# Three edits to a one-core transformer layer: separate PSUM banks in the seven-product quads, another order of the opening norms, earlier loads of the output projection's weights

## The chip, the cores and the metric

The kernel runs on one core of a Trainium2 chip. The metric is device time in microseconds (us); lower is better. The kernel before took 2078.35 us, the median of three runs (2078.32 to 2083.11).

## The reference

The kernel computes one layer of a hybrid decoder in float32: x of 1024 tokens by 1024 features, with 16 learned meta tokens ahead of them (1040 rows in all).

```python
h = h + 0.5 * swiglu(rms_norm(h, ffn1_norm), ffn1_w_in, ffn1_w_out)   # D_FF = 2816
u = rms_norm(h, mix_norm) @ w_in
o = concat[hgrn2(...4 heads, blocks of 128...), stick_breaking(...8 heads...)]
h = h + o @ w_out
h = h + 0.5 * swiglu(rms_norm(h, ffn2_norm), ffn2_w_in, ffn2_w_out)
# swiglu(h) = (silu(h @ w_in[:, :D_FF]) * (h @ w_in[:, D_FF:])) @ w_out
```

The output is h without the meta tokens.

## The kernel before, in words

**Products in three matmuls.** A float32 operand is held as two parts: a rounded high part (`wh`, `xh`, made by ScalarE's copy to fp32r at L268, L145 or L518) and the rest (`wl`, `xl`, made by VectorE's subtraction at L270, L147 or L520). A product of a 128-row piece is three matmuls: high by high, low by high, high by low. In `fast_in` three bufs each of `wh` and `wl` (and eight of `raw` in the first FFN, six in the second) let weights be prepared up to three products ahead of TensorE.

**Seven-product quads.** A 2x2 block product of the FFN's first matrix (`quad` in `fast_in`) is made from seven block products in place of eight: left operands are weight blocks a11, a21, a22, a12 or sums of them (s1 = a21 + a22, s2 = s1 - a11, a11 - a21, a12 - s2, made by GpSimd at L283), right operands are `B11, B21, B22, T1, T2, T3, T4`. TensorE works in the order B11, T2, B21, T3, T1, T4, B22; in quads that were begun early ("opened") the B11 and B21 products of six quads come first, and then T2, T3, T1, T4, B22 of one quad after the other. Each product is 12 matmuls and goes to a PSUM bank `qa` (B11, then B21 on top of it), `qb` (T2, then T3 and T4 on top of it) or `qc` (T1, then B22 on top). PSUM has two bufs each of `qa`, `qb`, `qc` and `qd`. VectorE or ScalarE reads a bank between two products that add up in it: `p1` is ScalarE's copy of B11 (L356), `u2 = p1 + qb` after T2 and `u3 = p1 + qb` after T3 (both L361). A matmul that adds to a bank waits until that read is over.

**The opening.** Tokens are in three blocks: block 0 of 272 columns ("plain", its products are ordinary ones into `qd`), blocks 1 and 2 of 384 columns each (the two halves of the quads). `run()` loads block 0's rows, norms them (`norm_rows`: per 128-row tile a square-sum, on VectorE for the second tile (L662) and else on ScalarE (L666), a square root on ScalarE (L667), a reciprocal (L670) and a multiplication of the row (L671) on VectorE), turns them by transposes on TensorE (L648) and makes `X`. Then 40 plain products of block 0 run (5 pairs of gate and up columns, L313 `qd<-X`), and between them, after products 12, 14, 16 and so on, six transposes of block 2's rows (evicted as `ba`, L692), then of block 1's (`bb`), while ScalarE and VectorE make the operands B and T (L219, L220, L705 to L718).

**What sets the order.** TensorE's order is written by hand (`manual_schedule(engines={nc.tensor.engine})`). ScalarE, VectorE, GpSimd and the DMA queue of SyncE are ordered by a list scheduler ahead of the run, by priority and by its own estimate of when things are ready; `high_priority()` raises a piece of code, and `issue_after(x)` puts it behind instruction x on its engines. On the chip each engine then goes strictly through its own list.

**The output projection.** `mix_out` runs first with the last four 128-row pieces of w_out (stick-breaking heads), which adds into `res` (L1640), then with the first four (the HGRN2 heads), which adds into `hm` (L1670). The weights of a half row of columns are four `raw` tiles (two bufs), cast at L145 and L147 into eight bufs of `wh` and `wl`. `ws[1]` are the weights of the second half of the columns, wanted from the third group of 12 matmuls of the second run on. HGRN2 head 3 is the last one; its output is `oH` (L965 on ScalarE, L966 on GpSimd) and is the fourth piece of each group. `from_dram` loads the `oT` tiles of the first run, two DMAs for each block.

Of the kernel before, what the change touches and what calls it, by code (L numbers as in the profile page):

```python
# [15 lines left out]
AF = mybir.ActivationFunctionType  # L16
# [4 lines left out]
P = 128  # L21
# [18 lines left out]
class Block:  # L40
# [212 lines left out]
    def fast_in(self, ops, n, w_in, actD, openers, ev0, open_ev, feed=None, plain=None,  # L253
# [19 lines left out]
        def block(i, h, col):  # L273
            t = self.wraw.tile([P, 4, P], F32, tag="raw", name="raw", bufs=self.in_bufs)
            nc.sync.dma_start(
                t, w_in[512 * h : 512 * h + 512, col + P * i : col + P * i + P]
                .rearrange("(k p) f -> p k f", p=P)
            )
            return t
# [58 lines left out]
        def quad(col, take, opened=None, also=None):  # L338
# [41 lines left out]
            u3 = kept("u3", p1, go("b", "T3", False))  # L380
            take(1, 1, go("c", "T1", True), u3)
            take(1, 0, go("b", "T4", False), p1)
# [273 lines left out]
    def norm_rows(self, ci, rows, junk):  # L656

        nc = self.nc
        for i, (row, at, m) in enumerate(rows):
            s, r = self.ss[:m, 3 * ci + i, 0:1], self.ss[:m, 3 * ci + i, 1:2]  # L660
            if i == 1:
                nc.vector.scalar_tensor_tensor(  # L662
                    junk[1][:m], row[:m], 1.0, row[:m], ALU.mult, ALU.mult, accum_out=s
                )
            else:
                nc.scalar.activation(junk[0][:m], row[:m], AF.Square, accum_out=s)  # L666
            self.root = nc.scalar.activation(  # L667
                r, s, AF.Sqrt, bias=self.eps[:m], scale=1.0 / D
            )
            nc.vector.reciprocal(r, r)  # L670
            nc.vector.tensor_scalar_mul(row[:m], row[:m], r)  # L671

    def first_plain(self, rows, junk, x):
# [3 lines left out]
        def evict(k, ps):  # L677
            g = self.g1[:, k : k + 1]
            hi, lo = x[0][:, k, :], x[1][:, k, :]
            nc.scalar.mul(hi, ps, g)  # L680
# [77 lines left out]
    def hgrn_fill(self, xh, xl, pool, dst):  # L758

        nc = self.nc  # L760
        nc.scalar.activation(self.lb, self.mx, AF.Sigmoid)
        nc.scalar.activation(self.lbc, self.mx, AF.Sigmoid, scale=-1.0)
# [574 lines left out]
    def run(self):  # L1337
# [20 lines left out]
        with ExitStack() as c0:  # L1358
            with ExitStack() as c1:
                with tc.manual_schedule(engines={nc.tensor.engine}), ExitStack() as c2:  # L1360
# [37 lines left out]
                    rows.append(self.rows_of(2, rp, nc.sync))  # L1398
                    drain(islice(steps, 4))
                    self.norm_rows(2, rows[1], junk)  # L1400
# [3 lines left out]
                    rows.append(self.rows_of(1, rp, nc.sync))  # L1404
                    self.norm_rows(1, rows[2], junk)
# [205 lines left out]
            with tc.manual_schedule(engines={nc.tensor.engine}):  # L1611
                right, cx, pre = ExitStack(), ExitStack(), ExitStack()
                with ExitStack() as c1:
# [10 lines left out]

                    def from_dram(b):
                        t = self.pool_o.tile([P, 2, 4, P], F32R, tag="oT", name="oT", bufs=3)
                        for i in range(2):
                            self.last_o = nc.sync.dma_start(
                                t.bitcast(F32)[:, i],
                                oD[:, :, i, b * P : b * P + P].rearrange("k p t -> p k t"),  # L1630
                            )
# [40 lines left out]
                    with tc.issue_after(self.last_o.ins):  # L1672
                        for b in range(2):
                            begin(0, b)
                        ws[1] = self.mix_weights(0, 1)
# [153 lines left out]
```

## Time and profile before

| | |
|---|---|
| median of three runs | 2078.35 us |
| lowest and highest run | 2078.32 and 2083.11 us |
| the profiled execution: its own time | 2084.77 us |
| the profiled execution: span from first to last instruction | 2083.1 us |
| TensorE busy | 2012.5 us (97%) |
| VectorE, ScalarE, GpSimd busy | 1377.7, 909.3, 636.5 us |
| mean granted TensorE clock | 0.995 |

The profile is one execution. Its rows give the start in us, a duration, the engine (PE is TensorE, PEld its weight loads, DVE VectorE, ACT ScalarE, POOL GpSimd, SPq SyncE's DMA queue), the line of the kernel, the operation, out and in, and in square brackets how long the engine had been idle and what released it. TensorE sets the time of nearly all stages; where it is idle or its clock is lowered, time is lost.

### The profile page before, as it was taken

Reading aid. Unit: us, or ns where it says so; the run is one execution under the profiler, and the core shown is the slowest. Engines: PE = TensorE matmul, PEld = TensorE weight load, DVE = VectorE, ACT = ScalarE, POOL = GpSimd, SP = SyncE. Lnnn points to the kernel's source line nnn. Section 1 sums busy time; section 2 is a strip of 40 time slices with the busy share of each in tenths; the row PEclk is TensorE's granted clock in tenths of the full one; section 3 lists DMA queues with packets and bytes.
Section 4 is the critical chain, followed back from the end, with each engine's and each line's share of the span. In section 5 each row is a group of like instructions: output and inputs, shape, how many; then the busy total and the mean of one; then the engine's idle time right before and its main releaser. Section 6 shows DMA issues by size and latency. Waiting matters only on the chain.

```text
span 2083.1 us, 31612 instructions
## 1 busy us (share of the span) xinstructions
PE 2012.5 (97%) x11249; PEld 1787.1 (86%) x11249; DVE 1377.7 (66%) x2073; ACT 909.3 (44%) x1864; POOL 636.5 (31%) x696
## 2 busy tenths in 40 slices
PE   7899999999999999999999998999999999999999
PEld 7899999999987899988887878878778888878887
DVE  6767754546688842257878757648667667667774
ACT  7743333334564534456566624336223323334443
POOL 2256644452000002243433300210555445431000
PEclk9999999999999999999999999999999999999999
DMA  8453322226875745435453262674333333239573
GB/s 240 134 179 114 110 93 85 96 86 213 282 219 172 234 134 168 150 116 131 123 140 108 68 215 92 203 258 132 105 123 107 96 107 112 91 138 351 188 227 112
DMA packets 289647, 314.96 MB, mean 151 GB/s; under 512 B 24080, under 2 KB 218000, under 8 KB 289488
## 3 DMA queue, kind: packets, MB, share of 16 engines
q1 hardware_dynamic: 272304, 260.83, 40.4%
q0 software_dynamic: 16144, 52.10, 6.6%
q8 instruction: 89, 1.46, 0.3%
q14 instruction: 70, 0.57, 0.1%
q10 hardware_dynamic: 1040, 0.00, 0.0%
HBM read 228.62 MB, written 84.23 MB: 150 GB/s over the span
## 4 chain that ended last, share of the span: by engine, by line
PE 78%; DVE 5%; ACT 2%; issue 1%; DMA 1%; POOL 0%; SPq 0%; DVEq 0%; ACTq 0%; POOLq 0%
PE o L599 17%; PE qb L313 13%; PE qc L313 8%; PE qa L313 8%; PE proj L162 5%; PE proj L160 5%; PE proj L161 5%; PE qd L313 3%; PE wo L1252 3%; PE o L561 3%; PE flip L1071 2%; PE lvl L840 2%; DVE keep L1217 1%; PE oacc L1141 1%; PE oacc L1143 1%
## 5 line engine op out<-in xcount | busy, mean ns | idle before, releaser
L313 PE MATMUL qb<-T,wh 128*128 128x384 f32 (+1 forms) x1056 | 319.7, 363 | 8.8 <-DVE u L361 8.7
L270 DVE TENSOR_TENSOR wl<-s,wh 128x512 fp32r<-128x512 f32 x176 | 199.4, 1133 | 96.4 <-ACT wh L268 92.7
L313 PEld LDWEIGHTS qb<-T,wh 128*128 128x128 f32 x1056 | 195.7, 188 | 34.3 <-ACT wh L268 11.9
L313 PE MATMUL qa<-B,wh 128*128 128x384 f32 (+1 forms) x704 | 213.9, 367 | 0.3 <-ACT sg L415 0.3
L599 PE MATMUL o<-wl,th 128*128 128x512 f32 x539 | 209.7, 391 | 3.4 <-DVE wl L520 3.4
L268 ACT CAST wh<-s 128x512 fp32r<-128x512 f32 x176 | 109.5, 622 | 231.7 <-PE qb L313 170.3
L599 PE MATMUL o<-wh,tl 128*128 128x512 f32 x539 | 209.6, 390 | 0.7 <-DVE tl L520 0.7
L599 PE MATMUL o<-wh,th 128*128 128x512 f32 x539 | 210.0, 391 | 0.0
L160 PE MATMUL proj<-xh,wh 128*128 128x384 f32 (+2 forms) x576 | 206.0, 358 | 0.2 <-ACT xh L250 0.2
L270 DVE TENSOR_TENSOR wl<-raw,wh 128x512 fp32r<-128x512 f32 x184 | 170.0, 927 | 50.6 <-ACT wh L268 47.0
L161 PE MATMUL proj<-xh,wl 128*128 128x384 f32 (+2 forms) x576 | 200.1, 347 | 0.0
L162 PE MATMUL proj<-xl,wh 128*128 128x384 f32 (+2 forms) x576 | 199.9, 347 | 0.1
L268 ACT CAST wh<-raw 128x512 fp32r<-128x512 f32 x184 | 113.6, 620 | 189.3 <-PE qc L313 100.6
L313 PE MATMUL qb<-T,wl 128*128 128x384 f32 (+1 forms) x528 | 191.9, 363 | 0.0
L518 ACT CAST th<-act 128x512 fp32r<-128x512 f32 (+2 forms) x176 | 96.5, 550 | 179.0 <-PE o L599 121.8
L520 DVE TENSOR_TENSOR tl<-act,th 128x512 fp32r<-128x512 f32 (+2 forms) x176 | 105.7, 603 | 65.6 <-ACT th L518 64.2
L283 POOL TENSOR_TENSOR s<-raw 128x512 f32<-128x512 f32 x88 | 122.0, 1387 | 82.6 <-DVE wl L270 67.5
L313 PE MATMUL qd<-X,wh 128*128 128x272 f32 x704 | 145.1, 293 | 1.6 <-DVE X L681 1.2
L313 PEld LDWEIGHTS qa<-B,wh 128*128 128x128 f32 x704 | 130.5, 188 | 16.5 <-ACT sg L415 0.7
L1217 DVE TENSOR_TENSOR_SCAN keep<-keep 128x144 f32<-128x144 f32 (+6 forms) x112 | 127.2, 1138 | 8.6 <-ACT keep L1213 6.0
L1222 POOL TENSOR_TENSOR sig<-sig,keep 128x144 f32<-128x144 f32 (+3 forms) x64 | 88.1, 1377 | 145.1 <-DVE keep L1217 72.6
L313 PE MATMUL qa<-B,wl 128*128 128x384 f32 (+1 forms) x352 | 128.7, 366 | 0.3 <-DVE wl L270 0.3
(342 smaller groups left out, 4778.3 us busy)
## 6 DMA issues: line engine op xcount, KB each, us to landing
raw<-in_ffn_w_in_dram SPq DMA_DIRECT2D x228, 256.0 KB, 3.1
raw<-in_ffn_w_out_dram SPq DMA_DIRECT2D x176, 256.0 KB, 4.2
raw<-in_w_in_dram SPq DMA_DIRECT2D x28, 512.0 KB, 4.2
ks<-kD SPq DMA_DIRECT2D x32, 260.0 KB, 5.4
oT<-oD SPq DMA_DIRECT2D x32, 256.0 KB, 4.5
ak<-in_ffn_w_out_dram SPq DMA_DIRECT2D x22, 256.0 KB, 5.1
v<-vD SPq DMA_DIRECT2D x8, 576.0 KB, 4.9
vD<-vhl SPq DMA_DIRECT2D x8, 512.0 KB, 4.0
```

The source lines that it names most:

```text
L160: nc.tensor.matmul(ps, wh[:, s], xs, start=k == 0, stop=False)
L161: nc.tensor.matmul(ps, wl[:, s], xs, start=False, stop=False)
L162: nc.tensor.matmul(ps, wh[:, s], xl[:, k, c0 : c0 + n], start=False, stop=k == nk - 1)
L268: nc.scalar.copy(hi, src)
L270: nc.vector.tensor_sub(lo, src, hi.bitcast(F32))
L283: op(t, x, y)
L313: nc.tensor.matmul(ps, a[:, k, :], b[:, k0 + k, :], start=start and k == 0 and i == 0, stop=k == 3 and i == 2, skip_group_check=True,)
L518: nc.scalar.copy(hi, src)
L520: nc.vector.tensor_sub(lo, src, hi.bitcast(F32))
L599: nc.tensor.matmul(banks[bank][m], z[:, m * P : (m + 1) * P], y, start=start and q == 0 and e == 0, stop=q == nq - 1 and e == 2, skip_grou ...
L1217: nc.vector.tensor_tensor_scan(out=kv, data0=kv, data1=kv, initial=1.0 if last else keep[:, end : end + 1], op0=ALU.mult, op1=ALU.bypass,)
L1222: nc.gpsimd.tensor_mul(sig, sig, keep[:, 1 : nk + 1])
```

## The change

There are four edits.

1. In a quad, T2, T3 and T4 each start a bank of `qb` of their own. `u3` is now `u2` plus T3's bank, and the fourth result is `u3` plus T4's bank. The number of instructions is the same.
2. The norms of the two wide blocks (2 and 1) are written earlier in the program, at high priority, their row loads behind a certain weight load, their arithmetic behind a certain eviction or the root before. One square root and one reciprocal serve the three tiles of a block. In block 0, the third tile of 16 rows has its square on VectorE in place of the second.
3. The two sigmoids of the HGRN2 lower bound are put behind the last ScalarE copy of a B11 product of the first FFN.
4. The weights `ws[1]` of the output projection are loaded behind the fifth from last `oT` load, and not behind the last one.

```diff
-            nc.sync.dma_start(
+            self.last_w = nc.sync.dma_start(
                 t, w_in[512 * h : 512 * h + 512, col + P * i : col + P * i + P]
...
-            u3 = kept("u3", p1, go("b", "T3", False))
+            u3 = kept("u3", u2, go("b", "T3", True))
             take(1, 1, go("c", "T1", True), u3)
-            take(1, 0, go("b", "T4", False), p1)
+            take(1, 0, go("b", "T4", True), u3)
...
-    def norm_rows(self, ci, rows, junk):
-
-        nc = self.nc
-        for i, (row, at, m) in enumerate(rows):
-            s, r = self.ss[:m, 3 * ci + i, 0:1], self.ss[:m, 3 * ci + i, 1:2]
-            if i == 1:
+    def norm_rows(self, ci, rows, junk, whole=False):
+
+        nc = self.nc
+        sums = self.ss[:, 3 * ci : 3 * ci + 3]
+
+        def square(i, row, m):
+            s = sums[:m, i, 0:1]
+            if i == (1 if whole else 2):
                 nc.vector.scalar_tensor_tensor(
                     junk[1][:m], row[:m], 1.0, row[:m], ALU.mult, ALU.mult, accum_out=s
                 )
             else:
                 nc.scalar.activation(junk[0][:m], row[:m], AF.Square, accum_out=s)
+
+        def root(m, i):
+            r = sums[:m, i, 1]
             self.root = nc.scalar.activation(
-                r, s, AF.Sqrt, bias=self.eps[:m], scale=1.0 / D
+                r, sums[:m, i, 0], AF.Sqrt, bias=self.eps[:m], scale=1.0 / D
             )
             nc.vector.reciprocal(r, r)
-            nc.vector.tensor_scalar_mul(row[:m], row[:m], r)
+
+        for i, (row, at, m) in enumerate(rows):
+            square(i, row, m)
+            if not whole:
+                root(m, slice(i, i + 1))
+                nc.vector.tensor_scalar_mul(row[:m], row[:m], sums[:m, i, 1:2])
+        if whole:
+            root(P, slice(0, 3))
+            for i, (row, at, m) in enumerate(rows):
+                nc.vector.tensor_scalar_mul(row, row, sums[:, i, 1:2])
...
-            nc.scalar.mul(hi, ps, g)
+            self.last_x = nc.scalar.mul(hi, ps, g)
...
-        nc.scalar.activation(self.lb, self.mx, AF.Sigmoid)
-        nc.scalar.activation(self.lbc, self.mx, AF.Sigmoid, scale=-1.0)
+        with self.tc.issue_after(self.last_p1.ins):
+            nc.scalar.activation(self.lb, self.mx, AF.Sigmoid)
+            nc.scalar.activation(self.lbc, self.mx, AF.Sigmoid, scale=-1.0)
...
                     drain(islice(steps, 4))
-                    rows.append(self.rows_of(2, rp, nc.sync))
+                    with tc.high_priority():
+                        with tc.issue_after(self.last_w.ins):
+                            rows.append(self.rows_of(2, rp, nc.sync))
+                        with tc.issue_after(self.last_x.ins):
+                            self.norm_rows(2, rows[1], junk, True)
                     drain(islice(steps, 4))
-                    self.norm_rows(2, rows[1], junk)
+                    with tc.high_priority():
+                        with tc.issue_after(self.last_w.ins):
+                            rows.append(self.rows_of(1, rp, nc.sync))
+                        with tc.issue_after(self.root.ins):
+                            self.norm_rows(1, rows[2], junk, True)
                     ba, bb = [], []
                     for _ in self.first_block(2, rows[1], rp, "ba", ops, ba):
                         drain(islice(steps, 2))
-                    rows.append(self.rows_of(1, rp, nc.sync))
-                    self.norm_rows(1, rows[2], junk)
...
+                    loads = []
                     def from_dram(b):
...
-                            self.last_o = nc.sync.dma_start(
+                            loads.append(nc.sync.dma_start(
...
-                    with tc.issue_after(self.last_o.ins):
+                    with tc.issue_after(loads[-5].ins):
+                        ws[1] = self.mix_weights(0, 1)
+                    with tc.issue_after(loads[-1].ins):
                         for b in range(2):
                             begin(0, b)
-                        ws[1] = self.mix_weights(0, 1)
```

ScalarE's list in the opening, between the last B operand of block 2 and the first `bb` eviction of block 1 (`wh` is a plain product's weight, `sp` the gate of a plain product, `junk` a square, `ss_x` a root). Before:

```order
L667 ACT_TABLE_LOAD
L667 ACTIVATE ss_x<-ss_x,eps 128x1
L268 CAST wh<-raw 128x512
L394 ACT_TABLE_LOAD
L394 ACTIVATE sp<-qd 128x272
L666 ACTIVATE junk_228,ss_x<-row 128x1024
L761 ACT_TABLE_LOAD
L761 ACTIVATE lb<-mx 128x4
L667 ACT_TABLE_LOAD
L667 ACTIVATE ss_x<-ss_x,eps 128x1
L762 ACT_TABLE_LOAD
L762 ACTIVATE lbc<-mx 128x4
```

And in the changed kernel, first the place where block 1's root now stands, behind the first two `ba` evictions:

```order
L706 ACTIVATE ba_567<-xps,g_69 128x384
L706 ACTIVATE ba_571<-xps,g_69 128x384
L668 ACTIVATE junk_228,ss_x<-row 128x1024
L268 CAST wh<-raw 128x512
L672 ACT_TABLE_LOAD
L672 ACTIVATE ss_x<-ss_x,eps 128x3
```

and then, in the same list, the place of the rows shown of before:

```order
L219 CAST B_204<-ba_736 128x384
L394 ACTIVATE sp<-qd 128x272
L706 ACTIVATE bb_787<-xps,g_69 128x384
L706 ACTIVATE bb_789<-xps,g_69 128x384
```

Between the last B operand and the first `bb` there is now one gate; the table loads, the roots, the sigmoids and the square have gone from there, and the last square and the root of block 1 stand ahead of all B operands.

TensorE's list does not change in its matmuls; what changes is on what the first matmul of a product waits. In an opened quad of the second FFN (`T_15736` is T2, `T_15734` T3, `T_15732` T1, `T_15730` T4), before:

```order
L313 MATMUL qb<-T_15736,wh 128x512 [waits Activation_49]
L313 MATMUL qb<-T_15736,wl 128x512 [waits DVE_49]
L313 MATMUL qb<-T_15734,wh 128x512 [waits DVE_49,Activation_49]
L313 MATMUL qc<-T_15732,wh 128x512 [waits Activation_49]
L313 MATMUL qb<-T_15730,wh 128x512 [waits DVE_49,Activation_49]
```

And in the changed kernel (T2 is `T_15772`, T3 `T_15770`, T1 `T_15768`, T4 `T_15766`):

```order
L313 MATMUL qb<-T_15772,wh 128x512 [waits Activation_49]
L313 MATMUL qb<-T_15772,wl 128x512 [waits DVE_49]
L313 MATMUL qb<-T_15770,wh 128x512 [waits Activation_49]
L313 MATMUL qb<-T_15770,wl 128x512 [waits DVE_49]
L313 MATMUL qc<-T_15768,wh 128x512 [waits Activation_49]
L313 MATMUL qc<-T_15768,wl 128x512 [waits DVE_49]
L313 MATMUL qb<-T_15766,wh 128x512 [waits DVE_49,Activation_49]
```

The first matmul of T3 waits for its weight's high part only; VectorE is waited for by the second, which needs the low part.

SyncE's queue at the end of the first run of the output projection (`oT` and `res` feed the first run, `hm` and `raw<-in_w_out_dram` the second). Before:

```order
L1636 DMA res<-h1N 128x512
L1628 DMA oT<-oD 128x4x128 x2
L1636 DMA res<-h1N 128x512
L1628 DMA oT<-oD 128x4x128 x2
L1666 DMA hm<-hmN 128x1024 x2
L1636 DMA res<-h1N 128x512
L140 DMA raw<-in_w_out_dram 128x512 x2
L1666 DMA hm<-hmN 128x1024
L140 DMA raw<-in_w_out_dram 128x512 x2
```

And in the changed kernel:

```order
L140 DMA raw<-in_w_out_dram 128x512 x2
L1659 DMA res<-h1N 128x512
L1651 DMA oT<-oD 128x4x128 x2
L1659 DMA res<-h1N 128x512
L1651 DMA oT<-oD 128x4x128 x2
L1689 DMA hm<-hmN 128x1024 x2
L1659 DMA res<-h1N 128x512
L1689 DMA hm<-hmN 128x1024
L140 DMA raw<-in_w_out_dram 128x512 x2
```

The first two weight loads moved ahead of two `res` loads, four `oT` loads and two `hm` loads; ScalarE's, VectorE's and TensorE's lists there are as before.

More of the change, by code (lines that the diff above doesn't have):

```diff
@@ L1627, in from_dram @@
                         for i in range(2):
-                            self.last_o = nc.sync.dma_start(
+                            loads.append(nc.sync.dma_start(
                                 t.bitcast(F32)[:, i],
                                 oD[:, :, i, b * P : b * P + P].rearrange("k p t -> p k t"),
-                            )
+                            ))
                         return t[:, 0], t[:, 1]
```

## The prediction

> **What bounds the kernel now.** I read the page, then the waits of TensorE, then the timeline and the windows of the three places that the change touches.
>
> ```profile
> span 2083.1 us, 31612 instructions
> PE 2012.5 (97%) x11249; PEld 1787.1 (86%) x11249; DVE 1377.7 (66%) x2073; ACT 909.3 (44%) x1864; POOL 636.5 (31%) x696
> ```
> ```profile
> PE xps L648 <- DVE row L671: 8.1, 2, 5.9
> PE qb L313 <- DVE u L361: 8.7, 9, 1.1
> PE wo L1252 <- ACT oH L965: 1.1, 1, 1.1
> PE wo L1252 <- POOL oH L966: 0.6, 1, 0.6
> PE wo L1252 <- DVE res L1640: 0.7, 1, 0.7
> ```
>
> TensorE is idle for 2083.1 - 2012.5 = 70.6 us and sets the time everywhere else, so only idle time of TensorE, or time at a lowered clock, can be won. The change can reach five of its waits, 19.2 us in sum, and what the clock loses behind them. I take them place by place.
>
> **The opening.** Six transposes and the next product normally follow each other at once (46.54 to 47.11: 0.57 us). At 50.22 they don't:
>
> ```profile
> 46.54 0.82 PE L648 MATMUL xps<-ident,row 128*128 128x128 f32 x6
> 47.11 0.37 PE L313 MATMUL qd<-X,wh 128*128 128x272 f32 x1
> ...
> 50.22 0.38 PE L648 MATMUL xps<-ident,row 128*128 128x128 f32 x2
> ...
> 59.12 0.69 PE L648 MATMUL xps<-ident,row 128*128 128x128 f32 x2 [5.94 <-DVE row L671]
> 59.46 0.57 PE L313 MATMUL qd<-X,wh 128*128 128x272 f32 x1
> ```
> ```profile
> 55.00:60.00 5.00, 0.88 (x4) 0.88 (x5) 0.92 (x2) 4.90 (x7) 0.00 (x0) 0.50 0.11 32
> 60.00:65.00 5.00, 5.00 (x27) 5.00 (x26) 2.79 (x6) 2.32 (x6) 0.00 (x0) 0.56 0.00 0
> ...
> 70.00:75.00 5.00, 5.00 (x43) 5.00 (x42) 5.00 (x12) 4.97 (x11) 0.23 (x1) 1.00 0.60 179
> ```
>
> The hole costs 59.46 - (50.22 + 0.57) = 8.7 us. Behind it the clock column reads 0.56, and 27 matmuls run where 43 do at full clock: 16 x 5.00/43 = 1.9 us. What filled the hole is ScalarE's list:
>
> ```profile
> 50.12 1.28 ACT L667 ACT_TABLE_LOAD   x1
> ...
> 54.98 1.28 ACT L761 ACT_TABLE_LOAD   x1
> 56.27 0.20 ACT L761 ACTIVATE lb<-mx 128x4 f32<-128x4 f32 x1
> ...
> 59.63 1.05 ACT L692 ACTIVATE bb<-xps,g 128x384 f32<-128x384 f32 x2
> ```
>
> In the changed list these roots stand ahead of the B operands and the sigmoids are gone, so block 1's rows are normed long before 50 us, and the hole and the low clock go: 10.6 us. That is what TensorE could win; the other two engines must let it. ScalarE: before its list reaches the place of 50.12 it now has one square and an accumulator read more (some 1.2 us) and two roots fewer (0.6 us), with five table loads as before. It has no slack there, so `bb` starts near 50.8, not 59.63. VectorE is 5.00 of 5.00 busy from 70 on:
>
> ```profile
> 60.24 1.03 DVE L705 TENSOR_TENSOR ba<-bb,ba 128x384 f32<-128x384 f32 x2 [1.18 <-ACT bb L692]
> ...
> 90.53 0.68 DVE L270 TENSOR_TENSOR wl<-raw,wh 128x512 fp32r<-128x512 f32 x1
> ```
>
> From its first operand of block 1 to the weights of the last plain product are 31.0 us, with 2.2 us idle in the window 60 to 65. The same work begins about 51.3 and needs at least 28.8: it ends at 80.1 in place of 91.2, 11.1 us sooner. So both sides say about 10.6 to 11. Against it stands the load of block 1's last tile, now issued behind the twentieth weight load, near 31 us by the places of these loads before, and a square on ScalarE waits for it, with the weight casts behind:
>
> ```profile
> row<-in_x_dram SPq DMA_DIRECT2D x7, 512.0 KB, 5.6
> ```
>
> By 5.6 us it lands near 36.6, some 1.5 us later than ScalarE gets there; most of that eats the start, which is about 1 us earlier since the first tile's multiplication no longer stands behind the second tile's square. I take **10.5** (bounds 7, if the landing and VectorE both cost 1.5 to 2; 13, if the early start is kept as well).
>
> [...]
>
> **The quads.** Six of the nine `u` waits are in the opened quads of the second FFN, where T3 follows T2 at once:
>
> ```profile
> 1472.34 0.39 PE L313 MATMUL qb<-T,wh 128*128 128x512 f32 x1
> 1473.61 0.47 PE L313 MATMUL qb<-T,wh 128*128 128x512 f32 x1 [0.88 <-DVE u L361]
> ```
> ```profile
> 1472.77 0.69 DVE L361 TENSOR_TENSOR u<-qb,p 128x512 f32<-128x512 f32 x1 [0.43 <-PE qb L313]
> ```
>
> T3 starts 1.27 us behind T2's last matmul; matmuls of this width follow each other at 0.23. With its own bank T3 waits for its weights alone, which ScalarE and VectorE had three products earlier. 6 x 1.04 = 6.2 us. The other three waits are T4's in the first FFN:
>
> ```profile
> 131.74 3.51 DVE L270 TENSOR_TENSOR wl<-raw,wh 128x512 fp32r<-128x512 f32 x1 [1.08 <-ACT wh L268]
> 135.18 0.54 DVE L361 TENSOR_TENSOR u<-qb,p 128x384 f32<-128x384 f32 x1
> ```
> ```profile
> 135.87 0.41 PE L313 MATMUL qb<-T,wh 128*128 128x384 f32 x1 [1.03 <-DVE u L361]
> ```
>
> Here VectorE itself is late: the 3.51 us subtraction is T4's own low part, over at 135.25, so the second matmul still waits for it; the `u` that T4 no longer waits for ends 0.5 us later. 3 x 0.4 = 1.2 us. Together **7.5** (bounds 4, if T3's weights turn out to be just in time; 8.7, all nine waits).
>
> **The output projection.**
>
> ```profile
> 1360.90 1.00 SPq L1628 DMA_DIRECT2D oT<-oD  x2
> ...
> 1373.70 1.57 SPq L140 DMA_DIRECT2D raw<-in_w_out_dram  x2
> ```
> ```profile
> 1381.75 0.62 ACT L145 CAST wh<-raw 128x512 fp32r<-128x512 f32 x1 [6.76 <-DMA raw<-in_w_out_dram]
> 1382.27 0.61 ACT L965 CAST oH<-attn 128x512 fp32r<-128x512 f32 x1
> ```
> ```profile
> 1377.28 1.41 DVE L960 SCALAR_TENSOR_TENSOR attn<-onp,og,KB 128x512 f32<-128x512 f32 x2 [0.70 <-PE onp L958]
> ```
> ```profile
> 1379.61 0.40 PE L1252 MATMUL wo<-wh,oH 128*128 128x512 f32 x1
> ...
> 1381.45 0.39 PE L1252 MATMUL wo<-wh,oH 128*128 128x512 f32 x1
> ...
> 1382.94 0.50 PE L1252 MATMUL wo<-wh,oH 128*128 128x512 f32 x1 [1.10 <-ACT oH L965]
> ...
> 1385.45 0.80 PE L1252 MATMUL wo<-wh,oH 128*128 128x512 f32 x1 [0.65 <-DVE res L1640]
> ...
> 1388.91 0.63 PE L1252 MATMUL wo<-wh,oH 128*128 128x512 f32 x2
> ```
>
> ScalarE stands at a weight cast until the load of 1373.70 lands, and `oH`, whose input was there at 1378.7, stands behind it; GpSimd's half of `oH` and VectorE's `res` follow late, and the matmuls from 1385.45 to 1388.91 run slowly. 20 matmuls take 9.3 us where 20 x 0.23 = 4.6 would do: 4.7 us. The loads now stand at the `oT` pair of 1360.90 (the rows of the order above), issue near 1362 and land before 1375 even at the 8 us they took; the casts then wait for `wh` bufs that the first run gives up around 1377 and 1378, ahead of `oH`. `oH` starts near 1378.1, and TensorE needs it at 1381.7. I take **4.5** (bounds 1, if the cast now waits for its buf as long as for the load; 4.7).
>
> **The sigmoids** cost 1.28 + 0.2 + 0.2 = 1.7 us of ScalarE at their new place, between two casts where it was idle for 2.33 us waiting for TensorE:
>
> ```profile
> 486.22 0.62 ACT L268 CAST wh<-raw 128x512 fp32r<-128x512 f32 x1 [2.33 <-PE qd L313]
> ```
>
> I take **0**; without that cover it would be up to 1.7.
>
> **Sum.** 10.5 + 7.5 + 4.5 = 22.5 us. The profiled execution took 2084.77 us (span 2083.1), which would become 2062.3. The median of the runs is 6.4 us below the profiled one: 2078.35 - 22.5 = **2056** us.
>
> **The rivals.**
>
> *ScalarE holds the opening.* For it: ScalarE and VectorE have hardly a gap in 31 to 50 us and 70 to 90 us, and the square for block 1's last tile now stands in front of weight casts. Against it: fewer table loads in the whole opening. If that load lands 3 us later than 5.6 and the low clock stays (1.9), and each weight cast behind it is late, the opening keeps 4: 22.5 - 6.5 = 16, **2062**.
>
> *The wait at `oH` only moves* to the `wh` bufs or GpSimd: 1 of 4.5 remains, 19 in all, **2059**. Against it: TensorE's last use of those bufs is before 1379.6.
>
> *VectorE is as late for weights as it was for `u`*: the quads give 1, 16 in all, **2062**. Against it: T3's weights are three products old.
>
> *Nothing sticks in the opening and the projection* (the order moves, the end of VectorE's work does not): only the quads' 7.5 less 1.7 for the sigmoids, **2073**.
>
> [...]
>
> **How the numbers follow.** Forecast 0.70, ScalarE holds 0.12, `oH` moves 0.08, late weights 0.04, nothing sticks 0.03, slower 0.03. A measurement here can tell some 0.3%, 6.2 us, from no change. Faster by more: the first four, 0.94; within: 0.03; slower: 0.03. The terms' upper bounds sum to 26.4 (2052), the lower ones to 12 (2066), and the runs of one kernel spread over 4.8 us (2078.32 to 2083.11), so the range is 2050 to 2066; it leaves out the last two cases.
>
> **What would show it.** In the changed profile: no wait on `row` at the transposes beyond 2 us, clock 1.00 from 45 to 65, the first quad's `qa` near 83 us in place of 93.97; no `qb <- u` wait in the second FFN and 14 to 14.7 us per opened quad cut to 13.7; `oH` casts at about 1378 on the old time scale, without the three `wo` waits. Wrong would make it: ScalarE idle on `row<-in_x_dram` for over 3 us, VectorE's `wl` named as releaser of `qd`, or new waits of TensorE in the quads.

## The result, and the profile after

The changed kernel takes 2063.2 us (median of six runs, 2061.22 to 2064.07), the kernel before, run beside it, 2082.57 us (six runs, 2078.32 to 2084.76). The ratio of the two, estimated over the runs side by side, is 0.9909, 95% interval 0.9896 to 0.9923: 18.9 us less, within 16 to 22 (the medians differ by 19.4). Savings in time further on go by such ratios. The forecast was 2056 us in a range of 2050 to 2066, from a sum of 22.5 us.

The head of the page of the changed kernel, and its waits of TensorE that answer to those quoted of before (us in total, times, longest):

```profile
span 2061.0 us, 31571 instructions
PE 2004.8 (97%) x11249; PEld 1782.3 (86%) x11249; DVE 1376.6 (67%) x2069; ACT 901.2 (44%) x1855; POOL 638.6 (31%) x696
```
```profile
PE xps L648 <- DVE row L681: 8.6, 2, 8.0
PE qc L313 <- DVE wl L270: 1.9, 1, 1.9
PE qd L313 <- DVE sp L397: 1.6, 1, 1.6
PE qd L313 <- DVE wl L270: 1.3, 2, 0.9
PE wo L1267 <- DMA oT<-oD: 1.0, 1, 1.0
PE wo L1267 <- DVE hm L1693: 0.6, 1, 0.6
```

All five waits that the change could reach are gone, `qb <- u` with all its nine. (The 8.0 us in the first row is the start of the kernel, which waits for its first data as before.) The last five rows are among the largest that now stand at the places the change touches. Two of them are not new: the wait of `qc` for `wl` was 1.4 us before, those of `qd` for `wl` 0.6 in sum.

The hole of the opening, seen in the windows of the changed kernel (length; busy time and count of TensorE, its weight loads, VectorE, ScalarE, GpSimd; granted clock; DMA):

```profile
45.00:50.00 5.00, 3.37 (x28) 3.16 (x28) 5.00 (x11) 4.98 (x10) 0.54 (x1) 1.00 0.61 159
50.00:55.00 5.00, 4.96 (x41) 4.71 (x40) 3.79 (x12) 4.75 (x11) 0.00 (x0) 1.00 0.62 183
55.00:60.00 5.00, 5.00 (x43) 5.00 (x42) 5.00 (x11) 4.56 (x10) 0.54 (x1) 1.00 0.57 165
60.00:65.00 5.00, 5.00 (x44) 5.00 (x43) 4.99 (x11) 4.76 (x11) 0.54 (x1) 1.00 0.55 158
```

TensorE does 43 matmuls where it did 4, at clock 1.00. In place of the hole stands a wait of 1.6 us near 47.

By the tiles that they name, TensorE's 11249 matmuls stand in the same order in every trace of this study, so two traces can be laid side by side, matmul by matmul, and each stretch of TensorE's list has a length of its own in each trace. The two profiles differ by 22.0 us at the last matmul: 0.4 lost in the first 17 us, 8.2 won from there to the first quad, 1.0 in the quads of the first FFN, 3.2 in the later part of the mixers (1064 to 1350 us of before, code that was not changed), 2.9 in the output projection, 7.1 in the opened quads of the second FFN, and 0.1 less in all else.

### The profile page after: what moved, and what is told of

It reads as the page before. It is cut to its first block, busy times and chain, and to the rows that moved or that the text cites. A ratio compares the mean times of both kernels' runs of the same rounds, so it can differ in the third digit from the quotient of the medians.

```text
span 2061.0 us, 31571 instructions
## 1 busy us (share of the span) xinstructions
PE 2004.8 (97%) x11249; PEld 1782.3 (86%) x11249; DVE 1376.6 (67%) x2069; ACT 901.2 (44%) x1855; POOL 638.6 (31%) x696
## 4 chain that ended last, share of the span: by engine, by line
PE 83%; DVE 7%; DMA 3%; ACT 3%; issue 2%; POOL 0%; SPq 0%; DVEq 0%; POOLq 0%; ACTq 0%
PE o L599 16%; PE qb L313 15%; PE qa L313 10%; PE qc L313 10%; PE proj L162 5%; PE proj L160 5%; PE proj L161 5%; PE qd L313 4%; PE o L561 3%; PE wo L1267 3%; PE flip L1086 2%; DVE wl L270 1%; PE lvl L855 1%; DVE keep L1232 1%; PE oacc L1156 1%
```

## The experiments

All were run with the kernel before beside them. For the stretches I give one table behind the experiments; each kernel's profile gives one row.

**The parts alone.** Three kernels have one part each, the rest as before.

```diff
-            u3 = kept("u3", p1, go("b", "T3", False))
+            u3 = kept("u3", u2, go("b", "T3", True))
...
-            take(1, 0, go("b", "T4", False), p1)
+            take(1, 0, go("b", "T4", True), u3)
```

> Only the seven-product quads: T3 and T4 get a bank of their own, the opening and the output projection as before. Theory (the parts are local and add up): with the matmuls of the two profiles laid side by side, the six opened quads of the second FFN give 1.0 to 1.3 us each, 7.0 in sum, and the three waits of the first FFN give 1.1 each and lose 0.6 to 0.8 of it again within twelve matmuls, because VectorE's weight part is late there, so some 8.0 us in the profile; no qb wait on u is left. Rival A (VectorE is as late for weights as it was for u): 1 to 2 us. [...]

Measured: ratio 0.9973 (0.9961 to 0.9985), 5.6 us less. In the profile the six opened quads give 7.1 us and no `qb <- u` wait is left; rival A falls for the second FFN. In the first FFN, where the theory had some 1 us less, the stretch is 0.7 us longer than before. The windows of this kernel show why:

```profile
195.23:198.64 3.41, 1.58 (x9) 1.26 (x9) 3.41 (x2) 0.77 (x2) 3.21 (x5) 1.00 0.34 108
198.64:202.05 3.41, 3.41 (x12) 3.41 (x12) 2.03 (x3) 0.00 (x0) 2.76 (x2) 0.50 0.41 135
```

TensorE comes sooner to a weight part of VectorE's that is late, so its wait there grows. In the waits of the kernel before, and then of this one:

```profile
PE qc L313 <- DVE wl L270: 1.4, 1, 1.4
```
```profile
PE qc L313 <- DVE wl L270: 1.8, 1, 1.8
```

The longer wait leaves TensorE only 1.58 us of work in a stretch of 3.41 us (0.46 of it), and the next 3.41 us run at clock 0.50, with 12 matmuls in them. In the profile before, the emptiest 3.41 us around this wait (from 194.22 on) have matmuls in 0.58 of them, and the clock stays at 1.00.

The second kernel has parts 2 and 3 of the change, the opening norms and the sigmoids. Its edit is that of the change, from which these are two lines:

```diff
...
-                    self.norm_rows(2, rows[1], junk)
...
+                            self.norm_rows(2, rows[1], junk, True)
...
```

> Only the opening (early norms, one root per block, sigmoids moved); quads and output projection as before. Theory: the hole of 8.7 us at 50.2 and the low clock behind it go, a new wait of 1.6 us near 47 stays, some 8.4 us in all, first qa near 85.5. Rival (the gain of the opening in the combined kernel leans on the new banks of the quads, since the first quads start in its tail): under 6 us.

Measured: ratio 0.9970 (0.9959 to 0.9982), 6.2 us less. The first `qa` is at 84.8 us, and the waits show the old ones of the quads and the new one near 47:

```profile
PE qb L313 <- DVE u L361: 8.6, 9, 1.1
...
PE qd L313 <- DVE sp L397: 1.6, 1, 1.6
```

The opening does not lean on the quads: that rests on the first `qa`, since the timed 6.2 us (3.7 to 8.5) fit the theory's 8.4 as well as the rival's less than 6.

How far single profiles can be compared here: five of them have exactly this opening (this one, the two of the changed kernel and the two with other loads for the output projection), and their first `qa` is at 84.8 to 86.8 us. Counted from TensorE's 41st matmul, which leaves out how long the first data took, it comes 67.5 to 68.9 us later in these five, and 74.9 to 77.1 us later in the three profiles with the old opening.

The third kernel has part 4, the loads of the output projection.

```diff
-                    with tc.issue_after(self.last_o.ins):
+                    with tc.issue_after(loads[-5].ins):
+                        ws[1] = self.mix_weights(0, 1)
+                    with tc.issue_after(loads[-1].ins):
                         for b in range(2):
                             begin(0, b)
-                        ws[1] = self.mix_weights(0, 1)
```

> Only the second pair of output-projection weights issued sooner. Theory: the three waits (2.4 us) and the spell of low clock behind them (1.7 us) go, 1.0 to 1.4 come back as a wait for the last oT pair and 0.6 as one for hm: 2 to 2.6 us net in the profile, which the timed runs can hardly tell from 0. Rival (the wait for oT in the combined kernel has another cause than these loads, such as the work arriving earlier): 3.5 to 4.5 us net, no wait for oT.

Measured: ratio 0.9987 (0.9978 to 0.9996), 2.7 us less; the stretch is 3.4 us shorter than in the first profile, 1.7 of it the spell of low clock. The three waits are gone, a wait for `oT` is not there, and one for `hm` has come:

```profile
PE wo L1252 <- DVE hm L1672: 1.5, 1, 1.5
```

The 3.4 us lie between the theory's 2 to 2.6 and the rival's 3.5 to 4.5, and the timed 2.7 us (0.8 to 4.6) fit either. The rival is right that the `oT` wait does not belong to these loads. The `hm` wait does not come from them either: the two kernels above, with the old loads, have it too (1.0 and 1.1 us).

The three parts alone sum to 14.5 us by their ratios, each uncertain by 1.9 to 2.5, the whole change to 18.9 with 2.8: the difference of 4.4 us lies just within these uncertainties taken together (4.8), so no gain is lost or made by their meeting that these runs could show.

**The late row load in the opening.** ScalarE stood idle for the last tile of block 1, and its first `bb` came at 54.16:

```profile
38.91 1.06 ACT L668 ACTIVATE junk<-row 128x1024 bf16<-128x1024 f32 x1 [2.19 <-DMA row<-in_x_dram]
...
54.16 1.06 ACT L706 ACTIVATE bb<-xps,g 128x384 f32<-128x384 f32 x2
```

```diff
-            self.load_rows(eng, row, r0, m)
+            self.load_rows(self.nc.scalar if ci == 1 and r0 == c0 + 2 * P else eng, row, r0, m)
...
+                        last_w = self.last_w
                     drain(islice(steps, 4))
                     with tc.high_priority():
-                        with tc.issue_after(self.last_w.ins):
+                        with tc.issue_after(last_w.ins):
```

> The changed kernel, with the load of block 1's last tile issued from ScalarE's own queue, right behind a weight cast near 30 us, in place of SyncE's at 33.5. Theory (the opening fell short of 10.5 us because this load came 2.2 us too late for its square, and the casts and TensorE's two products behind it were late): the load lands near 36, the idle 2.2 us on ScalarE and the 1.6 us wait of TensorE near 47 go, first qa 1.5 to 2.1 us sooner, near 83.5 to 84. Rival (VectorE's multiplications of rows between the weight parts hold the stretch 42 to 50 us in any case): qa within 0.5 us of 85.5.

Measured: ratio 0.9918 (0.9900 to 0.9937), not to be told from the changed kernel. The load was issued at 29.95 and its square ran at 36.45 without a wait; TensorE's wait near 47 is gone as well. But the first `qa` is at 85.2, and TensorE waits five us later, for ScalarE's evictions:

```profile
46.80 0.82 PE L648 MATMUL xps<-ident,row 128*128 128x128 f32 x6
...
52.38 0.77 PE L648 MATMUL xps<-ident,row 128*128 128x128 f32 x5 [1.07 <-ACT ba L706]
```

The load was late, as I had thought, and little hung on it: from the 41st matmul on, the first `qa` comes after 67.5 us, as in the quickest of the five profiles above, and 0.8 us sooner than in the profile of the changed kernel, where the theory had 1.5 to 2.1 us. The scheduler also ordered ScalarE's and VectorE's lists anew here, from about 31 us on, so this run does not show the load by itself.

**Work taken from either engine.** Two kernels built on the last one leave work out: in one the two squares of block 1 on ScalarE take 64 of 1024 columns, in the other VectorE's multiplications by the root do.

```diff
+                w = 64 if whole and ci == 1 else D
-                nc.scalar.activation(junk[0][:m], row[:m], AF.Square, accum_out=s)
+                nc.scalar.activation(junk[0][:m, :w], row[:m, :w], AF.Square, accum_out=s)
```

> The kernel of the run with the row load on ScalarE's queue, in which ScalarE's two squares of block 1 read 64 of 1024 columns (so these rows' norms are wrong): some 1.9 us of ScalarE less between 30 and 42 us. Theory (ScalarE's list holds the opening): the wait of TensorE near 52 us shrinks by 1 us or more and the first qa comes 1 to 1.9 us sooner than 85.2. Rival (VectorE's list holds it): qa within 0.5 us of 85.2.

```diff
-                nc.vector.tensor_scalar_mul(row, row, sums[:, i, 1:2])
+                w = slice(0, 64 if ci == 1 else D)
+                nc.vector.tensor_scalar_mul(row[:, w], row[:, w], sums[:, i, 1:2])
```

> The kernel of the run with the row load on ScalarE's queue, in which VectorE's three multiplications of block 1's rows by their root reach 64 of 1024 columns (so the other columns are not normed): some 1.9 us of VectorE less between 41 and 44 us. Theory (ScalarE's list holds the opening): first qa within 0.5 us of 85.2. Rival (VectorE's list holds it, since it has hardly a gap from 55 us on): qa 1 to 1.9 us sooner.

Measured, in one execution each: first `qa` at 87.2 and at 86.1, against 85.2. Less work on either engine made nothing sooner. In the first of them the scheduler also laid the lists out anew, and the wait on `sp` came back, so it does not say what ScalarE's squares are worth. In the second ScalarE's list is the same and VectorE's nearly so; TensorE's waits for ScalarE's evictions stay at 1.4 us and those for `wl` grow from 0.5 to 1.9. So VectorE's multiplications do not hold the opening; whether ScalarE's work between 30 and 42 us does is left open.

**The order of VectorE's list near 47.** The wait of 1.6 us was for a multiplication (`sp`) that frees a bank of TensorE's; the product it reads had ended near 43, and it stood behind four halvings:

```profile
46.22 1.96 DVE L220 TENSOR_TENSOR B<-ba,B 128x384 fp32r<-128x384 f32 x4
48.10 0.68 DVE L270 TENSOR_TENSOR wl<-raw,wh 128x512 fp32r<-128x512 f32 x1
48.70 0.43 DVE L397 TENSOR_TENSOR sp<-qd,sp 128x272 f32<-128x272 f32 x1
```

```diff
-                nc.vector.tensor_mul(sg[i], ps, sg[i])
+                with self.tc.high_priority():
+                    nc.vector.tensor_mul(sg[i], ps, sg[i])
```

> The changed kernel, in which VectorE's multiplications that free the banks of the plain products (sp) stand higher in its list: near 47 us one halving pair and more than five other instructions sooner. Theory (the 1.6 us wait of TensorE at 46.8 to 49.3 is the order of VectorE's list: the product was ready at 42.8, and its multiplication stood behind four halvings and the row multiplications): that wait goes, and if nothing else in the list decides, the first qa comes near 84. Rival (engine time: VectorE and ScalarE both need the whole stretch, so the wait only moves, as it did when the row load was moved): another wait of 1 to 2 us shows up within ten us, qa within 0.7 us of 85.5.

Measured: ratio 0.9907 (0.9891 to 0.9923), first `qa` at 85.1. The wait is gone, and again one has come behind it:

```profile
51.79 1.24 PE L649 MATMUL xps<-ident,row 128*128 128x128 f32 x6 [1.19 <-ACT ba L707]
```

So list order was the cause of that wait, as the theory says, and by the first `qa` the rival is right on what it is worth. Counted from the 41st matmul the stretch has 67.1 us, 0.4 less than the quickest of the five profiles above, so some part of a microsecond may be there.

**One root for each block.**

```diff
-                            self.norm_rows(2, rows[1], junk, True)
+                            self.norm_rows(2, rows[1], junk)
...
-                            self.norm_rows(1, rows[2], junk, True)
+                            self.norm_rows(1, rows[2], junk)
```

> The changed kernel with the norms of the wide rows as early as now, but one root for each tile instead of one for each block (two more table loads on ScalarE in the opening, and four more roots and reciprocals). Theory (the place of the norms brings the gain, the single root saves ScalarE some 4 us in 30 to 45 us, which it has no slack for): half of the saving shows, first qa 1.5 to 3 us later than 85.5. Rival (one root for each block is what empties the hole): the hole near 50 comes back in part, first qa 5 us or more later. Second rival (the single root is worth nothing): within 0.5 us.

The edit also puts the square of the third tile on VectorE in place of the second's, and ScalarE has two table loads more in the opening. Measured: ratio 0.9924 (0.9907 to 0.9940), first `qa` at 85.4. The second rival holds: the place of the norms brings the gain, the merged root none that shows. (Here too the scheduler ordered the lists anew.) TensorE's waits have only moved ahead of 45 us; from there it has none:

```profile
45.00:50.00 5.00, 5.00 (x44) 5.00 (x43) 4.22 (x10) 5.00 (x12) 0.54 (x1) 1.00 0.68 200
50.00:55.00 5.00, 5.00 (x42) 5.00 (x42) 4.00 (x8) 4.82 (x12) 0.00 (x0) 1.00 0.52 151
```

**The sigmoids back.**

```diff
-        with self.tc.issue_after(self.last_p1.ins):
-            nc.scalar.activation(self.lb, self.mx, AF.Sigmoid)
-            nc.scalar.activation(self.lbc, self.mx, AF.Sigmoid, scale=-1.0)
+        nc.scalar.activation(self.lb, self.mx, AF.Sigmoid)
+        nc.scalar.activation(self.lbc, self.mx, AF.Sigmoid, scale=-1.0)
```

> The changed kernel with the two sigmoids where the kernel before had them, so two more table loads and two short activations (some 3 us of ScalarE) stand between the evictions of block 1. Theory (ScalarE's list is what holds the stretch of 45 to 60 us, and VectorE's from 60 on): the evictions are up to 3 us later and VectorE, which has no slack there, keeps 1.5 to 3 us of that, first qa near 87 to 88.5, and nothing changes at 486. Rival (ScalarE has slack behind 60 us, and VectorE alone decides): first qa within 0.5 us of 85.5.

Measured: ratio 0.9921 (0.9901 to 0.9941); first `qa` at 87.7, 2.2 us later than in the profile of the changed kernel. Windows of this kernel, and then of the changed one:

```profile
75.00:80.00 5.00, 5.00 (x42) 5.00 (x41) 5.00 (x11) 4.96 (x10) 0.86 (x1) 1.00 0.69 199
80.00:85.00 5.00, 3.26 (x24) 2.83 (x23) 5.00 (x4) 2.76 (x6) 4.03 (x3) 1.00 0.16 47
```
```profile
75.00:80.00 5.00, 5.00 (x42) 5.00 (x41) 5.00 (x11) 3.58 (x8) 0.91 (x2) 1.00 0.67 204
80.00:85.00 5.00, 5.00 (x42) 5.00 (x41) 5.00 (x9) 1.97 (x4) 4.92 (x2) 1.00 0.15 45
```

Four table loads are back, not the two that were expected (at 58.06, 64.66, 74.42 and 77.38 us, 1.28 us each): one ahead of each sigmoid and one ahead of the gate that follows it. With them ScalarE has hardly a gap up to 80 and TensorE runs dry at 80 to 85. From TensorE's 301st matmul to the first `qa` every other kernel with the new norms needs 31.5 us, this one 33.8. So that part of the change is worth 2.3 us, by what it takes out of the opening; the scheduler ordered the lists anew behind 58 us, which this run cannot part from the table loads. At its new place it costs nothing, as forecast: rows of the changed kernel's ScalarE, which still waits for TensorE behind it.

```profile
476.46 0.20 ACT L776 ACTIVATE lb<-mx 128x4 f32<-128x4 f32 x1
476.57 0.19 ACT L777 ACTIVATE lbc<-mx 128x4 f32<-128x4 f32 x1
477.47 0.62 ACT L268 CAST wh<-raw 128x512 fp32r<-128x512 f32 x1 [0.71 <-PE qd L313]
```

**The output projection once more.** Two kernels and one repeat.

```diff
-                    with tc.issue_after(loads[-5].ins):
+                    with tc.issue_after(loads[-1].ins):
                         ws[1] = self.mix_weights(0, 1)
```

> The changed kernel, with the second pair of output-projection weights issued right behind the last pair of oT loads instead of two pairs sooner (still ahead of the hm loads). Theory (the weight loads in front of them make the last oT pair late): the 1.0 us wait of TensorE for oT goes, the weights land near 1368 on the scale of the changed kernel, still ahead of the casts that need them, no wait on oH; 1.0 to 1.4 us less in the stretch of the projection. Rival (the oT pair is late because of its own place or of other traffic): the wait stays at about 1 us. Second rival (the weights now land too late): a wait on oH of 0.5 to 1.5 us comes back. [...]

Measured: ratio 0.9919 (0.9898 to 0.9940). The `oT` wait is gone, no wait on `oH` has come, and that on `hm` is 1.4 us. What VectorE stood for was the next load in line, the gain row of the second FFN; the row is from the repeat of the changed kernel, and profiles of the kernel before and of the projection alone have it too (0.49 and 2.55 us):

```profile
1385.03 1.28 DVE L238 SCALAR_TENSOR_TENSOR xn<-hm,rs,g2r 128x1024 f32<-128x1024 f32 x1 [1.63 <-DMA g2r<-in_ffn_norm_dram]
1386.23 1.28 DVE L1693 TENSOR_TENSOR hm<-wo,hm 128x512 f32<-128x512 f32 x2
```

The two waits go together: 13 profiles have this load at its old place. In 11 of them TensorE's wait on `hm` is VectorE's wait for the gain row less 1.0 to 1.1 us (from 0.6 behind 1.6 to 1.9 behind 3.0), and it is missing in the two in which VectorE waits 1.0 us or less.

```diff
-                    with tc.issue_after(loads[-5].ins):
+                    with tc.issue_after(loads[-1].ins):
                         ws[1] = self.mix_weights(0, 1)
+                    with tc.issue_after(loads[-1].ins):
+                        gain = self.gain_row(a["ffn2_norm"][0:1], hb, "g2r")
...
-                    gain = self.gain_row(a["ffn2_norm"][0:1], pn, "g2r")
```

> The changed kernel with the weight loads of the output projection behind the last oT pair, and the second FFN's gain row (g2r) loaded right behind them, ahead of the hm loads, instead of behind eight weight loads. Theory (what TensorE waits for last in the projection is g2r: VectorE stands at the first multiplication by it for 1.7 to 2.5 us and its sums of hm, which free TensorE's banks, stand behind that): no wait on oT and none on hm beyond 0.3 us; the stretch of the projection is 2 to 3 us shorter than in the changed kernel's profile, of the whole time some 0.1%. Rival (the hm loads themselves are late): a wait on hm of 0.6 to 1.9 us stays. [...]

Measured: ratio 0.9904 (0.9886 to 0.9922). No wait on `oT`, none on `hm`, as the theory says, and yet the stretch is 48.3 us long, between the 47.8 and the 48.9 of the two profiles of the changed kernel. ScalarE now stands 6.15 us for the last weights, and TensorE's only waits of the stretch by this view are these 0.4 us:

```profile
PE wo L1267 <- DVE wl L147: 0.4, 2, 0.2
```

Where the rest went shows beside the first profile of the changed kernel, matmul by matmul: this kernel wins 1.3 us where that one waits for `oT` and 0.9 where it waits for `hm`, and loses 1.5 us within nine matmuls from 1376.4 on. The two waits for `wl` are among these, and they follow each other up to 0.73 us apart where the usual pitch is 0.23. So the gain row was the cause of the `hm` wait, as the theory says, and the 2 to 3 us do not follow, since the weights are now what is late.

The changed kernel again, with no edit:

> The changed kernel as it is, once more, beside the kernel before. [...] Rival (the profiles' 22 us are the true gain, and the medians suffer from few runs): 0.9895 or less.

Measured: ratio 0.9910 (0.9892 to 0.9928), 18.7 us less (by the medians 16.2); the profiled span is 2064.9 us against 2061.0 for the same program. The rival's 0.9895 lies near the lower end of that interval. This profile has three spells of low clock that the first has not (0.51 at 190.50 to 193.91, 0.50 at 1074.63 to 1078.04 and at 1146.30 to 1149.70). Its projection has no `oT` wait at all:

```profile
PE wo L1267 <- DVE hm L1693: 0.6, 1, 0.6
```

So the 1.0 us for `oT` in the first profile was that execution's, not the program's (of the nine profiles with the loads at this place one more has it, with 0.7), and what the kernel with the later weight loads was made to remove was not there to be removed.

The stretches, in us, with the spells of halved clock (3.4 us each) inside them in brackets:

| kernel | first qa at | quads of FFN 1 | later part of the mixers | output projection | opened quads of FFN 2 | span |
|---|---|---|---|---|---|---|
| before | 94.0 | 139.8 (0) | 284.2 (2) | 51.8 (1) | 79.7 | 2083.1 |
| quads alone | 95.4 | 140.5 (1) | 281.9 (1) | 51.3 (0) | 72.5 | 2074.8 |
| opening alone | 84.8 | 139.6 (0) | 282.5 (1) | 48.9 (0) | 79.7 | 2069.2 |
| projection alone | 93.5 | 139.8 (0) | 282.7 (1) | 48.4 (0) | 79.6 | 2077.9 |
| changed | 85.5 | 138.8 (0) | 280.9 (0) | 48.9 (0) | 72.6 | 2061.0 |
| changed again | 86.8 | 140.3 (1) | 283.8 (2) | 47.8 (0) | 72.5 | 2064.9 |
| row load on ScalarE | 85.2 | 140.4 (1) | 280.9 (0) | 46.5 (0) | 72.6 | 2057.2 |
| weights behind oT | 84.9 | 138.7 (0) | 282.3 (1) | 47.8 (0) | 72.6 | 2057.7 |
| sigmoids back | 87.7 | 140.3 (1) | 283.2 (2) | 48.2 (0) | 72.6 | 2064.4 |
| short squares | 87.2 | 140.3 (1) | 282.3 (1) | 50.6 (0) | 72.6 | 2065.3 |
| short multiplications | 86.1 | 138.9 (0) | 280.9 (0) | 48.1 (0) | 72.6 | 2060.5 |
| sp first | 85.1 | 138.7 (0) | 282.5 (1) | 49.5 (0) | 72.6 | 2062.8 |
| root for each tile | 85.4 | 140.7 (1) | 283.8 (2) | 49.8 (0) | 72.6 | 2062.3 |
| gain row sooner | 86.1 | 140.3 (1) | 282.4 (1) | 48.3 (0) | 72.6 | 2062.8 |

The opened quads repeat to 0.1 us. The other stretches scatter by 1 to 4 us from one execution to the next; in the mixers that goes with the spells of low clock (280.9 without one, 283.2 to 284.2 with two). None of the variants is faster than the changed kernel beyond the intervals, and the two shortest spans (2057.2 and 2057.7) do not show in the medians (2063.58 and 2065.15).

## Why the prediction was right, and where it was wrong

The time lay in the range, and the direction and the likeliest case held; the gain was 18.9 us where the sum said 22.5. The time alone does not tell the cases apart: 2063.2 is nearer to three of the rivals (2062, 2062 and 2059) than to the forecast's 2056. The parts do. Part by part:

**The quads of the second FFN: right.** Forecast 6 x 1.04 = 6.2 us, measured 7.1 in every profile with the new banks. T3's first matmul now follows T2's last at the usual pitch; both stand in the middle row of the changed kernel's TensorE:

```profile
1457.26 0.39 PE L313 MATMUL qb<-T,wl 128*128 128x512 f32 x1
1457.49 0.61 PE L313 MATMUL qb<-T,wh 128*128 128x512 f32 x2
1457.94 0.39 PE L313 MATMUL qb<-T,wl 128*128 128x512 f32 x1
```

The term was 0.15 us a quad too small. The matmul behind the stall also ran longer (0.47 us in the row quoted of before, 0.39 here), which I had not counted; that gives 0.08 a quad. The rest is that two of the six waits were 1.02 us long and not 0.88. The prediction's "14 to 14.7 us per opened quad" was misread: T3 follows T3 at 14.7 to 14.9 us before, and at 13.6 now.

**The quads of the first FFN: the three waits right, what follows them left out.** Forecast 3 x 0.4 = 1.2; side by side each of the three waits gives 1.2 us and loses 0.7 to 0.8 of it within twelve matmuls, so some 0.5 stays. But the step left out what a wait that goes does to the next one. TensorE comes sooner to the `wl` that is late in any case, and that wait grows from 1.4 to 1.9 us, and the clock is halved for 3.4 us behind it in 7 of the 11 profiles with the new banks, and in none of the three without. Without the spell of low clock the stretch is 0.9 us shorter than before (138.8 against 139.7), with it 0.7 us longer. Over 11 profiles this part is worth nothing. The case "slower" did not come, but the clock did fall in a quad, once in each of those 7 profiles.

**The opening: mechanism right, 10.5 forecast, 8.5 measured** from the first `qa` of the two profiles, and 8.6 as the mean of five profiles with this opening against three without (8.0 of it behind the 41st matmul). Hole and low clock went as said (clock 1.00 from 45 to 65). The step that failed is "it has no slack there, so `bb` starts near 50.8": it starts at 54.16, and VectorE's first operand of block 1 comes at 54.77, not 51.3. I had allowed for a load that lands at 36.6. The load was issued at 33.48 and its square ran at 38.91; yet with that load moved the first `qa` came little sooner. What the sum lacked is that TensorE, freed of the hole, runs into its helpers elsewhere: between 20 and 55 us it is idle for 3.0 us in the changed kernel's profile, and for 1.0 us outside the hole in the one before. These are the 2 us that are missing. In the three variants that reached into this stretch (row load, `sp` first, root for each tile) it is 2.1 to 2.3 us, each time at another place (2.3 to 3.0 in the five profiles of the unchanged opening), and from 55 to 85 it is never idle in any of them. One wait removed by hand was followed by another each time; what would end all of them was not found.

**The output projection: 4.5 forecast, 2.9 in the profiles, and about 1.5 without the spell.** The three waits went, and the casts came as forecast, at 1378.0 on the old scale:

```profile
1367.13 0.62 ACT L980 CAST oH<-attn 128x512 fp32r<-128x512 f32 x1 [0.60 <-DVE attn L975]
```

What failed is the size. "20 matmuls take 9.3 us where 4.6 would do" took the waits and the 1.7 us of low clock of one execution for the program's. The eleven matmuls around these waits take 7.2 us in the profile before, and 5.2 and 4.3 in the two others with the old loads, neither of which has the spell; with the loads moved they take 2.5 (2.9 in one). So the term is 4.7 us in the execution it was read from, and 2.7 and 1.8 in the others. The rival "the wait at `oH` only moves" did not come: the wait on `hm` that now stands out (0 to 1.9 us) was there with the old loads too, 1.0 and 1.1 us in two of the three profiles, and goes with the gain row. The mean of nine profiles with the new place of the loads is 48.6 us (46.5 to 50.6), that of the three without it 50.7, or 50.1 with the spell taken off (48.9 to 51.3): the two sets overlap.

**The sigmoids: right**, 0 at the new place.

**The signs.** Of the signs of being wrong two came, in small: `wl` as releaser of `qd` (1.3 us in the profile of the changed kernel), and new waits of TensorE in the quads, such as

```profile
PE qb L313 <- DVE wl L270: 0.9, 3, 0.4
```

These are the T4 products, which now wait for their own low part where they waited for `u`. Of the signs of being right the first `qa` was off (85.5 us and not 83); the others came.

**What was not in the sum.** The later part of the mixers, which nobody touched, accounts for 3.2 of the 22.0 us between the two profiles: two spells of low clock (0.50 at 1081.56 to 1084.97 and at 1153.24 to 1156.65) that the first profile of the changed kernel happens not to have. The repeat has them. So the agreement of 22.0 with 22.5 is partly luck, and the timed 18.9 us is the better number: 8.6 for the opening, 7.1 for the opened quads and 1.5 to 2 for the projection make 17.2 to 17.7. The forecast also took the median of three runs, 2078.35, for the kernel's time; over the later batches the medians of the kernel before were 2080.9 to 2082.6.

## What to carry to other kernels

Lay the traces of two kernels side by side matmul by matmul before believing a difference of spans: unchanged stretches show at once how much of it is the execution's. A stall that is removed is worth what the next late thing leaves of it, so ask for each what TensorE then reaches sooner; here that was a weight part (and a lower clock), and two evictions in turn. A read between two products that add up in one PSUM bank was worth a bank of its own where the weights were ready: in the opened quads, the one part whose whole gain stayed, it won 1.2 us for each read removed.

## What the runs showed that had not been expected

**The clock fell behind stretches that were not idle.** The profile of the kernel before has four spells at clock 0.50 between its start and its end, one of 10.24 us that begins in the hole and three of 3.41 us. In the 3.41 us ahead of them matmuls filled 0.44 us (from 50.74 on), 1.48 (from 1078.15), 1.31 (from 1149.83) and 1.23 (from 1381.94). The share of matmuls in such a stretch does not tell by itself whether the clock falls: in the same profile it is 1.26 us in the 3.41 us from 1101.30 on, and the clock stays at 1.00. The same code of the mixers has a spell behind it in the kernel before (first fence) and in the repeat of the changed kernel (second), and none in the first profile of the changed kernel (third). There, 3.41 us from 1069.30 on, across the two windows shown, have 1.43 us of matmuls, and the clock stays at 1.00 behind them.

```profile
1078.15:1081.56 3.41, 1.48 (x11) 0.88 (x9) 3.38 (x5) 2.27 (x6) 0.26 (x2) 1.00 0.23 66
1081.56:1084.97 3.41, 3.36 (x15) 3.39 (x16) 2.14 (x4) 0.48 (x1) 1.67 (x2) 0.50 0.95 242
```
```profile
1071.21:1074.63 3.42, 1.48 (x11) 0.87 (x8) 3.39 (x5) 2.25 (x6) 0.26 (x2) 0.99 0.23 65
1074.63:1078.04 3.41, 3.38 (x16) 3.41 (x16) 2.14 (x4) 0.48 (x1) 1.68 (x2) 0.50 0.93 240
```
```profile
1068.10:1071.52 3.42, 2.15 (x18) 1.79 (x17) 3.42 (x3) 3.00 (x8) 1.34 (x2) 1.00 0.00 1
1071.52:1074.93 3.41, 2.71 (x23) 2.48 (x22) 3.18 (x6) 1.05 (x3) 0.76 (x1) 1.00 0.90 233
```

A spell cost about 1.5 us (mixers: 280.9 without one, 281.9 to 282.7 with one, 283.2 to 284.2 with two), and the two profiles of the changed kernel, which has no change between them, have none and three. The wait for `wl` in the quads shows the same: in the first profile of the changed kernel the 3.41 us from 185.70 on have 1.56 us of matmuls and the clock stays at 1.00, in the repeat those from 187.08 on have 1.59 and the clock behind them is 0.51. The wait of 1.6 us near 47 left it at 1.00 (1.78 us of matmuls in the 3.41 us from 47.50 on). What decides where a spell comes is left open here.

**One program, three to four us apart.** The same changed kernel has spans of 2061.0 and 2064.9 us, and its waits differ (1.0 us for `oT` in one and none in the other). A wait of 1 us in a single profile of this kernel is no property of the program until a second profile shows it.
